# Sliding-window attention in a hybrid decoder layer: the two key blocks of a query block merged into 128 columns a head

## The chip, the cores and the metric

The kernel runs on one core of a Trainium2 chip. The metric is the device time of one execution, in microseconds (us). Engines are named TensorE (PE in the profile; its weight loads are PEld), VectorE (DVE), ScalarE (ACT), GpSimd (POOL) and SyncE (SP), which issues the DMAs.

## The reference

One layer: a norm, a combined projection into a recurrent branch and an attention branch, a gated merge, an MLP and a per-layer embedding. What matters here is the attention, over 512 tokens in 4 blocks of 128, with 16 query heads of width 64 and 4 key and value heads:

```
kb = concat([previous block of k, own block of k])     # 256 keys for 128 queries
s = einsum(q, kb) * 64 ** -0.5
diff = 128 + qi - ci                                   # qi: query 0..127, ci: key 0..255
valid = (diff >= 0) & (diff < 128) & (key exists)
s = where(valid, s, -inf)
m = max(max(s), sink);  e = exp(s - m)
o = (e / (sum(e) + exp(sink - m))) @ vb
```

For a query `qi`, the valid keys are those of the previous block with index above `qi` and those of the own block with index up to `qi`: 128 of the 256, and of each pair of columns (c in the previous block, c in the own block) exactly one. The first block of queries has only its own key block.

## The kernel before

Activations have channels on the partitions and all 512 tokens as columns. Every matmul of a projection is done three times, with operands split into two parts (`mm3`, lines 144 to 147), with 512 columns each. Weights come in units of 128 x 1024 (512 KB), loaded by SyncE and split by ScalarE (`wh`, line 118) and VectorE (`wl`, line 119), up to three units ahead of use.

Attention is a loop (lines 568 to 600) of eight turns `u`: four query blocks for each half of the heads. A turn has two groups `g` of four heads. Between the steps of the attention stand the matmuls of two chunks of the gates' projections (`pgate`), 24 matmuls each, so that TensorE has work while the other engines compute a softmax. In a turn:

- `scores` (line 413) writes 4 heads x 256 columns into the PSUM tile `S`, which has one buffer.
- `softmax_max` (line 426): VectorE adds the mask to the scores, out of PSUM into the SBUF tile `sm` (line 431, two buffers), and takes the maximum over the columns (line 437); four small operations follow (lines 438 to 441).
- `softmax_exp` (line 444): ScalarE, four exponentials, one a head, with sums.
- `softmax_norm` (line 452): VectorE adds and inverts the denominators (lines 455, 456), GpSimd scales the four heads (line 458).
- `p_transpose` (line 462): TensorE transposes each head's 128 x 128 blocks, four heads of a key block into one PSUM tile `ppt` (line 467; the tag `tr` has two buffers, shared with the transposes of the queries).
- `p_evac` (line 471): the first key block's tile is copied to SBUF by ScalarE (line 475), the second's by VectorE (line 477).
- `pv` (line 480): products with v, accumulated over the key blocks; `o_split` (line 491) copies them out on ScalarE and VectorE.

For `u` = 0 and 4 the queries have one key block: there `window(u)` gives 1, the tiles are 128 columns a head, and one tile is transposed and copied. The transposes of the second group of turn `u` come in turn `u + 1`, behind the first gate chunk and ahead of the scores and the products with v. Those of the first group end its own turn.

The order of work on TensorE, ScalarE, SyncE and GpSimd is that of the code (line 80):

```
ctx.enter_context(tc.manual_schedule(engines={E.PE, E.Activation, E.SP, E.Pool}))
```

VectorE is not in that list: the framework orders its work when it builds the program, by priorities and modelled readiness.

The mask, with the rotary tables, is in the table `tab`, one DMA at the start (line 220) behind the loads of x and ahead of the next weights in SyncE's queue.

Of the kernel before, what the change touches and what calls it, by code (L numbers as in the profile page):

```python
# [24 lines left out]

# units of [128, 1024] in the packed weights, in order of use
U_QKV = 0
# [12 lines left out]

# columns of the packed per-channel vectors, 8 each
V_GMIX, V_GMLP, V_GPLE, V_CB, V_BRG, V_BIG, V_LAM, V_CW = 0, 8, 16, 24, 32, 40, 48, 56
N_VEC = 56 + 4 * 8


AHEAD = 3  # weight units split ahead of the one in use
F_BUFS = 24
W_BUFS = 4
N_WARM = 18
CUT = 6  # chunks of a gate projection before the turn of the next queries  # L50
LAG = 2  # chunks between a projection of the recurrent branch and its gates


def weight_order():
    """The units in order of use."""
    def run(u, n=KC):
        return list(range(u, u + n))

    o = run(U_QKV, 12) + run(U_GB) + run(U_GA)
    for m in range(KC + LAG):  # L60
        if m < KC:
            o.append(U_X + m)
        if m >= LAG:
            o.append(U_ATT + m - LAG)
    o += run(U_G) + run(U_RNN) + run(U_OUT) + run(U_MLP, 64) + run(U_PLE, 2) + run(U_PG)
    assert sorted(o + run(U_GATE, 2)) == list(range(N_UNITS))
    return o
# [3 lines left out]
def layer_kernel(ctx, tc, w_all, x_t, p_t, vecs, row, ctab, out_t):  # L71
# [5 lines left out]
    ps = ctx.enter_context(tc.tile_pool(name="ps", bufs=1, space=PSUM))  # L77
    # these engines run their instructions in the order in which they are written here
    E = mybir.EngineType
    ctx.enter_context(tc.manual_schedule(engines={E.PE, E.Activation, E.SP, E.Pool}))  # L80

    def rtile(name):
        """Both parts of four chunks of an activation."""
        return act.tile([P, 4, 2, S], F32R, tag="r", name=name, bufs=4)
# [15 lines left out]

# [1 line left out]
    order = weight_order()  # L102
# [20 lines left out]
    def wload(u):  # L123
        """Unit u, with the units that follow on their way."""
        while u not in ready or (order and len(ready) <= AHEAD):
            wissue()
        return ready.pop(u)

    def split(src, r):
        """r[:, 0] + r[:, 1] = src, both parts exact in 12 bits."""  # L130
        nc.scalar.activation(r[:, 0, :], src, AF.Copy)  # L131
        nc.vector.tensor_tensor(
            out=r[:, 1, :], in0=src, in1=r[:, 0, :].bitcast(F32), op=ALU.subtract
        )

    def split_scaled(src, scale, r):
        """The same for src * scale[partition]."""
        nc.scalar.activation(r[:, 0, :], src, AF.Copy, scale=scale)
        nc.vector.scalar_tensor_tensor(
            out=r[:, 1, :], in0=src, scalar=scale, in1=r[:, 0, :].bitcast(F32),  # L140
            op0=ALU.mult, op1=ALU.subtract,
        )
# [6 lines left out]
    def proj(out, w, acts, ks=range(KC), kcs=KC, w0=0, t=slice(0, S)):  # L149
        """out[c, t] = sum over k of w[k, c] * acts[k, t]."""  # L150
        wh, wl = w
# [4 lines left out]

# [1 line left out]
    vec = const.tile([P, N_VEC], F32, name="vec")  # L158
    nc.scalar.dma_start(vec, vecs)
    tab = const.tile([P, 512], F32, name="tab")  # L160
    rowb = const.tile([P, 144], F32, name="rowb")
    sinkb, qg, kg = rowb[:, 0:16], rowb[:, 16:80], rowb[:, 80:144]
    cosv = tab[:, 0:128].rearrange("p (n d) -> p n d", d=32)
    sinv = tab[:, 128:256].rearrange("p (n d) -> p n d", d=32)
    mask = tab[:, 256:512]
    ident = const.tile([P, P], F32, name="ident")
# [8 lines left out]

# [1 line left out]
    def rms_bcast(sqacc, name):  # L177
        """(mean over channels + eps) ** -0.5 for each token, on every partition."""
        pb = tr_ps(f"pb_{name}")
# [14 lines left out]
    def warm_up():  # L194
        """Keeps the tensor engine busy, and its clock up, until the first loads are in."""
        pw = tr_ps("pw")
        for _ in range(N_WARM):
            nc.tensor.matmul(pw[:, 0:P], ident, ident, start=True, stop=True)
# [6 lines left out]

# [1 line left out]
    xg = rtiles("xg")  # L207
# [13 lines left out]

# [1 line left out]
    att_scope = ExitStack()  # L223
# [4 lines left out]
    def qkv_group(grp, name, after=()):  # L228
        """Projections with tokens on the partitions; after[i]() is emitted behind part i."""
        banks = [mm_ps(f"{name}{n}") for n in range(NB)]  # L230
# [18 lines left out]
    def token_stats():  # L249
        """The mean squares with tokens on the partitions."""  # L250
        ptk = tr_ps("ptk")
# [8 lines left out]

    # rotary tables with the gains folded in: out = t * cc + swap_halves(t) * ss
    def rope_tables(gain, mul, name):
# [21 lines left out]
    def k_side(banks):  # L284
        """Normalized and rotated k of all tokens, v scaled by the norm of its token."""
        kraw = big("kraw")
# [42 lines left out]
    def k_split(kraw, n):  # L329
        # both parts, each doubled, so that a transpose fills all partitions  # L330
        k2 = att.tile([P, 2, 4, 2, HD], F32R, tag="qs", name=f"k2_{n}", bufs=2)
# [29 lines left out]
    def q_scale(u):  # L361
        """(sum of squares over a head + 64 eps mean(x^2)) ** -0.5"""
        n = u % NB
# [51 lines left out]
    def scores(u, g):  # L415
# [8 lines left out]
        return pss  # L424

    def softmax_max(u, g, pss):
        kv = 2 * (u // NB) + g
        w = window(u)[1] * P
        msk = mask[:, 2 * P - w : 2 * P]
        sm = big(f"sm{u}{g}")[:, :, :w]  # L430
        nc.vector.tensor_tensor(out=sm, in0=pss[:, :, :w],
                                in1=msk.unsqueeze(1).broadcast_to([P, 4, w]), op=ALU.add)
        st = att.tile([P, 4, 4], F32, tag="st", name=f"st{u}{g}", bufs=4)
# [28 lines left out]
    def p_transpose(u, g):  # L462
        sm, _ = probs[u, g]
        for kb in range(window(u)[1]):
            pt = tr_ps(f"ppt{u}{g}{kb}")
            for i in range(4):
                nc.tensor.transpose(pt[:, i * P : (i + 1) * P],
                                    sm[:, i, kb * P : (kb + 1) * P], ident)
            p_t_[u, g, kb] = pt

    def p_evac(u, g):
        for kb in range(window(u)[1]):
            prt = ftile(f"pt{u}{g}{kb}")
            if kb == 0:
                nc.scalar.activation(prt, p_t_[u, g, kb], AF.Copy)
            else:
                nc.vector.tensor_copy(prt, p_t_[u, g, kb])
            p_t_[u, g, kb] = prt
# [29 lines left out]

    # c4 = 4 * softplus(-lambda)
    lam = vec[:, V_LAM : V_LAM + 8]  # L510
# [9 lines left out]
    for d in (15, 13, 11, 9, 7, 5, 3):  # L520
        nc.vector.scalar_tensor_tensor(out=pl, in0=pl, scalar=1.0 / d, in1=s2,
                                       op0=ALU.add, op1=ALU.mult)
    # 4 * log1p(e) = 8 * s * (1 + pl)
    nc.vector.scalar_tensor_tensor(out=pl, in0=pl, scalar=1.0, in1=s_,
# [31 lines left out]

# [1 line left out]
    o = [rtile("o0"), rtile("o1")]  # L558
# [43 lines left out]

# [1 line left out]
    rnn = None  # L604
# [21 lines left out]
    def gate_weights(i):  # L626
        """The gates' weights of two chunks."""
        raw = wp.tile([P, S], F32, tag="wr", name=f"wrg{i}", bufs=2)
# [19 lines left out]
    def gate_post(m, xc, both):  # L648
        r, ig = both
        nc.gpsimd.tensor_tensor(out=ig, in0=ig, in1=xc, op=ALU.mult)  # L650
        # t = tanh(-log_a / 2); a = exp(log_a) = 1 - t (1 + a); sqrt(1 - a^2) = sqrt(t) (1 + a)
        nc.scalar.activation(xc, r, AF.Tanh, scale=cs[:, 0, m : m + 1])
# [22 lines left out]
    rnn_scope = ExitStack()  # L675
    later = [[], []]  # what is left of the recurrence, for the next two steps

# [75 lines left out]

# [1 line left out]
    def reload(m):  # L755
# [15 lines left out]

# [1 line left out]
    pr = ple.tile([P, 2, 2, S], F32R, name="pr")  # L773
# [29 lines left out]

# [1 line left out]
    es = []  # L805
# [32 lines left out]

# [1 line left out]
def _units(w):  # L840
    """[1024, 128 n] -> [n, 128, 8 * 128]: unit m holds columns 128 m.., k on the partitions."""
    import numpy as np
# [6 lines left out]
def _pack(i):  # L849
# [19 lines left out]
    for g in range(4):  # L869
# [10 lines left out]
    row = np.concatenate([i["sinks"][0], i["q_gain"][0], i["k_gain"][0]]).reshape(1, 144)  # L880
    # constants of the shapes: rotary angles and the window's mask
    inv = (10000.0 ** (-np.arange(0, 64, 2) / 64)).astype(np.float32)
    ang = np.arange(S, dtype=np.float32)[:, None] * inv[None, :]
    tabs = [t.reshape(NB, P, 32).transpose(1, 0, 2).reshape(P, 128)
            for t in (np.cos(ang), np.sin(ang))]
    qi, ci = np.arange(P)[:, None], np.arange(2 * P)[None, :]
    diff = P + qi - ci
    mask = np.where((diff >= 0) & (diff < P), 0.0, NEG).astype(np.float32)
    ctab = np.concatenate(tabs + [mask], axis=1).astype(np.float32)
    c = np.ascontiguousarray  # L890
# [20 lines left out]
```

## Time and profile before

| | |
|---|---|
| median of 3 runs | 861.26 us (861.09 to 861.58) |
| profiled execution | span 859.3 us from the first to the last instruction; 1.96 us below the median of the runs; no other time of it is recorded |
| busy share of the span | TensorE 99%, its weight loads 81%, VectorE 62%, ScalarE 42%, GpSimd 13% |
| the attention loop | about 83 to 226 us |
| granted TensorE clock | mean 0.999 |

A line of the groups view reads: line, engine, operation, tile written <- tiles read, shapes, count | busy us, mean ns of one | idle us of the engine before them, and what ended it. A line of the chain reads: start, length, what. A matmul's mean is a latency that overlaps its neighbours'. A line of the windows reads: the stretch and its length, then the busy time (and number of instructions) of PE, PEld, DVE, ACT and POOL, the granted clock, the share of the DMA engines and GB/s.

### The profile page before, as it was taken

Reading aid. Unit: us, or ns where it says so; the run is one execution under the profiler, and the core shown is the slowest. Engines: PE = TensorE matmul, PEld = TensorE weight load, DVE = VectorE, ACT = ScalarE, POOL = GpSimd, SP = SyncE. Lnnn points to the kernel's source line nnn. Section 1 sums busy time; section 2 is a strip of 40 time slices with the busy share of each in tenths; the row PEclk is TensorE's granted clock in tenths of the full one; section 3 lists DMA queues with packets and bytes.
Section 4 is the critical chain, followed back from the end, with each engine's and each line's share of the span. In section 5 each row is a group of like instructions: output and inputs, shape, how many; then the busy total and the mean of one; then the engine's idle time right before and its main releaser. Section 6 shows DMA issues by size and latency. Waiting matters only on the chain.

```text
span 859.3 us, 10186 instructions
## 1 busy us (share of the span) xinstructions
PE 851.2 (99%) x3922; PEld 698.9 (81%) x3922; DVE 530.6 (62%) x754; ACT 360.3 (42%) x578; POOL 113.1 (13%) x127
## 2 busy tenths in 40 slices
PE   9999999999999999999999999999999999999997
PEld 8878878777788878888888888888888888888886
DVE  4676787778578886776557643564346434655374
ACT  7342656565557787442434221222122212233431
POOL 2811343323111110000120000000000000002100
PEclk9999999999999999999999999999999999999999
DMA  6332212111223222333342332223223222222231
GB/s 238 122 98 74 74 50 74 63 62 50 75 86 110 74 74 94 117 130 127 136 146 84 98 122 93 81 98 102 98 95 98 98 99 98 98 94 93 84 123 50
DMA packets 25536, 83.35 MB, mean 97 GB/s; under 512 B 2960, under 2 KB 3344, under 8 KB 25488
## 3 DMA queue, kind: packets, MB, share of 16 engines
q1 hardware_dynamic: 25344, 82.66, 28.6%
q8 instruction: 31, 0.51, 0.2%
q14 instruction: 17, 0.14, 0.1%
q10 hardware_dynamic: 144, 0.05, 0.0%
HBM read 80.60 MB, written 2.10 MB: 96 GB/s over the span
## 4 chain that ended last, share of the span: by engine, by line
PE 80%; DVE 8%; ACT 6%; DMA 2%; issue 2%; POOL 1%; SPq 0%; ACTq 0%; DVEq 0%; POOLq 0%
PE pu L145 7%; PE pd L147 7%; PE pu L147 7%; PE pd L145 7%; PE pd L146 7%; PE pu L146 7%; PE pgate L145 3%; PE pgate L146 3%; PE pgate L147 3%; DVE xc L619 3%; DVE wl L119 2%; ACT wh L118 2%; PE S L421 2%; PE ppg L147 2%; PE ppg L145 2%; PE ppg L146 2%
## 5 line engine op out<-in xcount | busy, mean ns | idle before, releaser
L119 DVE TENSOR_TENSOR wl<-wr,wh 128x1024 fp32r<-128x1024 f32 (+1 forms) x143 | 179.8, 1258 | 55.9 <-ACT wh L118 55.8
L118 ACT ACTIVATE wh<-wr 128x1024 fp32r<-128x1024 f32 (+1 forms) x143 | 149.0, 1044 | 120.2 <-PE pd L146 96.2
L145 PE MATMUL pu<-x1g,wh 128*128 128x512 f32 x256 | 100.0, 391 | 0.0
L146 PE MATMUL pu<-x1g,wh 128*128 128x512 f32 x256 | 99.6, 389 | 0.0
L147 PE MATMUL pu<-x1g,wl 128*128 128x512 f32 x256 | 99.6, 389 | 0.0
L145 PE MATMUL pd<-u,wh 128*128 128x512 f32 x256 | 99.6, 389 | 0.0
L146 PE MATMUL pd<-u,wh 128*128 128x512 f32 x256 | 99.6, 389 | 0.0
L147 PE MATMUL pd<-u,wl 128*128 128x512 f32 x256 | 99.6, 389 | 0.0
L204 POOL TENSOR_TENSOR sq<-sq,sq_x 128x512 f32<-128x512 f32 x14 | 18.2, 1298 | 456.8 <-ACT sq_x L202 456.8
L131 ACT ACTIVATE u<-up 128x512 fp32r<-128x512 f32 x32 | 20.2, 632 | 126.5 <-DVE up L790 126.5
L799 DVE TENSOR_TENSOR xr<-pd,xr 128x512 f32<-128x512 f32 x32 | 22.1, 692 | 81.4 <-PE pd L147 81.4
L146 PEld LDWEIGHTS pu<-x1g,wh 128*128 128x128 f32 x256 | 48.1, 188 | 10.2 <-issue 0.2
L145 PEld LDWEIGHTS pu<-x1g,wh 128*128 128x128 f32 x256 | 48.1, 188 | 10.1 <-issue 0.2
L147 PEld LDWEIGHTS pu<-x1g,wl 128*128 128x128 f32 x256 | 48.1, 188 | 10.0
L146 PEld LDWEIGHTS pd<-u,wh 128*128 128x128 f32 x256 | 48.1, 188 | 10.0
L147 PEld LDWEIGHTS pd<-u,wl 128*128 128x128 f32 x256 | 48.1, 188 | 10.0
L145 PEld LDWEIGHTS pd<-u,wh 128*128 128x128 f32 x256 | 48.1, 188 | 9.9
L458 POOL TENSOR_SCALAR sm<-sm,st 128x256 f32<-128x256 f32 (+1 forms) x64 | 39.5, 633 | 96.1 <-DVE st L456 57.9
L145 PE MATMUL pgate<-xg,wh 128*128 128x512 f32 x128 | 51.3, 401 | 0.0
L147 PE MATMUL pgate<-xg,wl 128*128 128x512 f32 x128 | 50.1, 391 | 0.0
L146 PE MATMUL pgate<-xg,wh 128*128 128x512 f32 x128 | 50.1, 391 | 0.0
L789 DVE TENSOR_TENSOR up<-pu,rb_x 128x512 f32<-128x512 f32 x32 | 22.1, 691 | 40.0 <-PE pu L147 40.0
(225 smaller groups left out, 1704.6 us busy)
## 6 DMA issues: line engine op xcount, KB each, us to landing
wr<-in_w_all SPq DMA_DIRECT2D x141, 512.0 KB, 3.3
x<-in_x_t SPq DMA_DIRECT2D x8, 256.0 KB, 4.8
xr<-in_x_t SPq DMA_DIRECT2D x8, 256.0 KB, 3.6
out<-pgt SPq DMA_DIRECT2D x7, 256.0 KB, 2.1
wrg<-in_w_all SPq DMA_DIRECT2D x4, 256.0 KB, 2.9
wr<-in_w_all SPq DMA_DIRECT2D x2, 256.0 KB, 3.2
pk<-in_p_t SPq DMA_DIRECT2D x2, 256.0 KB, 3.7
tab<-in_ctab SPq DMA_DIRECT2D x1, 256.0 KB, 6.2
```

The lines of the kernel that those rows point to most:

```text
L118: nc.scalar.activation(wh[:, c], raw[:, c], AF.Copy)
L119: nc.vector.tensor_tensor(out=wl[:, c], in0=raw[:, c], in1=wh[:, c].bitcast(F32), op=ALU.subtract)
L131: nc.scalar.activation(r[:, 0, :], src, AF.Copy)
L145: nc.tensor.matmul(out, ah, bh, start=start, stop=False)
L146: nc.tensor.matmul(out, ah, bl, start=False, stop=False)
L147: nc.tensor.matmul(out, al, bh, start=False, stop=stop)
L204: nc.gpsimd.tensor_tensor(out=acc, in0=acc, in1=t, op=ALU.add)
L421: nc.tensor.matmul(pss[:, i, :], q_t[u, g][:, i, :], kt[part][:, kv, b0 * P : b0 * P + 256], start=part == 0, stop=part == 1)
L458: nc.gpsimd.tensor_scalar(out=sm[:, i, :], in0=sm[:, i, :], scalar1=den[:, i : i + 1], scalar2=1.0, op0=ALU.mult, op1=ALU.mult)
L619: nc.vector.scalar_tensor_tensor(out=xc[:, sft:], in0=xb[:, : S - sft], scalar=col(V_CW + 8 * j, m), in1=xc[:, sft:], op0=ALU.mult, op1=AL ...
L789: nc.vector.tensor_tensor(out=y, in0=pu, in1=r1, op=ALU.mult)
L799: nc.vector.tensor_tensor(out=x1[m], in0=pd, in1=x1[m], op=ALU.add)
```

## The change

The scores of a two-block group are merged into 128 columns a head: ScalarE copies the own block's columns, VectorE overwrites those where the key index is above the query index with the previous block's (a predicated copy). Maximum, exponentials and scaling then work on 128 columns a head. There is one transposed tile for a group. From it VectorE makes two SBUF tiles, one for each key block, by multiplying with a transposed 0/1 mask. The products with v are as before. For `u` = 0 and 4 a masking add and a copy by ScalarE stay. The table grows from 512 to 768 columns. Comments are removed as well.

```diff
-    tab = const.tile([P, 512], F32, name="tab")
+    tab = const.tile([P, 768], F32, name="tab")
-    mask = tab[:, 256:512]
+    neg, after = tab[:, 256:384], tab[:, 384:512]
+    keep = tab[:, 512:640], tab[:, 640:768]
...
+    def heads4(m):
+        return m.unsqueeze(1).broadcast_to([P, 4, P])
     def softmax_max(u, g, pss):
         kv = 2 * (u // NB) + g
-        w = window(u)[1] * P
-        msk = mask[:, 2 * P - w : 2 * P]
-        sm = big(f"sm{u}{g}")[:, :, :w]
-        nc.vector.tensor_tensor(out=sm, in0=pss[:, :, :w],
-                                in1=msk.unsqueeze(1).broadcast_to([P, 4, w]), op=ALU.add)
+        sm = big(f"sm{u}{g}").rearrange("p a b -> p (a b)")[:, 0 : 4 * P]
+        sm = sm.rearrange("p (i c) -> p i c", c=P)
+        if u % NB:
+            nc.scalar.activation(sm, pss[:, :, P : 2 * P], AF.Copy)
+            nc.vector.copy_predicated(sm, heads4(after.bitcast(mybir.dt.int32)), pss[:, :, 0:P])
+        else:
+            nc.vector.tensor_tensor(out=sm, in0=pss[:, :, 0:P], in1=heads4(neg), op=ALU.add)
...
     def p_transpose(u, g):
         sm, _ = probs[u, g]
-        for kb in range(window(u)[1]):
-            pt = tr_ps(f"ppt{u}{g}{kb}")
-            for i in range(4):
-                nc.tensor.transpose(pt[:, i * P : (i + 1) * P],
-                                    sm[:, i, kb * P : (kb + 1) * P], ident)
-            p_t_[u, g, kb] = pt
+        pt = tr_ps(f"ppt{u}{g}")
+        for i in range(4):
+            nc.tensor.transpose(pt[:, i * P : (i + 1) * P], sm[:, i, :], ident)
+        p_t_[u, g] = pt
     def p_evac(u, g):
-        for kb in range(window(u)[1]):
+        pt = p_t_.pop((u, g))
+        n = window(u)[1]
+        for kb in range(n):
             prt = ftile(f"pt{u}{g}{kb}")
-            if kb == 0:
-                nc.scalar.activation(prt, p_t_[u, g, kb], AF.Copy)
+            if n == 1:
+                nc.scalar.activation(prt, pt, AF.Copy)
             else:
-                nc.vector.tensor_copy(prt, p_t_[u, g, kb])
+                nc.vector.tensor_tensor(out=prt.rearrange("p (i t) -> p i t", t=P),
+                                        in0=pt.rearrange("p (i t) -> p i t", t=P),
+                                        in1=heads4(keep[kb]), op=ALU.mult)
             p_t_[u, g, kb] = prt
...
-    mask = np.where((diff >= 0) & (diff < P), 0.0, NEG).astype(np.float32)
-    ctab = np.concatenate(tabs + [mask], axis=1).astype(np.float32)
+    qi, ci = np.arange(P)[:, None], np.arange(P)[None, :]
+    own = ci <= qi
+    ctab = np.concatenate(tabs + [np.where(own, 0.0, NEG), ~own, ~own.T, own.T],
+                          axis=1).astype(np.float32)
```

## Rows read from the trace of the kernel before

**Rows 1.** The page: span, busy engines, chain by engine.
```profile
span 859.3 us, 10186 instructions
...
PE 851.2 (99%) x3922; PEld 698.9 (81%) x3922; DVE 530.6 (62%) x754; ACT 360.3 (42%) x578; POOL 113.1 (13%) x127
...
PE 80%; DVE 8%; ACT 6%; DMA 2%; issue 2%; POOL 1%; SPq 0%; ACTq 0%; DVEq 0%; POOLq 0%
```

**Rows 2.** Windows: two turns of the loop (u = 2, 3), the stage behind it.
```profile
113.40:131.64 18.24, 17.99 (x98) 13.94 (x98) 14.46 (x30) 11.83 (x31) 6.40 (x9) 1.00 0.18 60
131.64:149.20 17.56, 17.56 (x98) 13.93 (x98) 14.66 (x30) 10.68 (x29) 6.57 (x9) 1.00 0.18 62
226.00:318.00 92.00, 91.83 (x405) 75.40 (x403) 73.18 (x92) 62.50 (x84) 10.22 (x6) 1.00 0.27 92
```

**Rows 3.** The chain that ended last, 117 to 318 us: start, length, what.
```profile
117.88 2.70 POOL sm L458 x4
...
120.62 0.77 PE ppt L467 x5
121.39 0.94 PE S L421 x8
122.33 1.87 PE po L486 x8
...
130.76 0.87 PE ppt L467 x8
...
165.88 0.44 PE ppt L467 x4
...
226.14 0.61 ACT o L494
...
317.91 0.50 PE pg L145
```

**Rows 4.** Groups by line and shape, 82 to 226 us.
```profile
L447 ACT ACTIVATE sm<-sm,st,sc 128x256 f32<-128x256 f32 x48 | 28.2, 591 | 5.9 <-DVE st L441 5.9
...
L467 PE MATMUL ppt<-ident,sm 128*128 128x128 f32 x112 | 16.0, 275 | 0.6
L431 DVE TENSOR_TENSOR sm<-S,tab 128x1024 f32<-128x1024 f32 x12 | 14.6, 1220 | 5.7 <-PE S L421 5.7
L437 DVE TENSOR_REDUCE st<-sm 128x4 f32<-128x1024 f32 x12 | 14.5, 1210 | 0.1
...
L475 ACT ACTIVATE pt<-ppt 128x512 f32<-128x512 f32 x16 | 9.4, 590 | 31.7 <-PE ppt L467 31.6
...
L477 DVE COPY pt<-ppt 128x512 f32<-128x512 f32 x12 | 8.2, 687 | 11.7 <-PE ppt L467 11.7
...
L447 ACT ACTIVATE sm<-sm,st,sc 128x128 f32<-128x128 f32 x16 | 7.7, 487 | 0.0
...
L431 DVE TENSOR_TENSOR sm<-S,tab 128x512 f32<-128x512 f32 x4 | 2.8, 689 | 4.7 <-PE S L421 4.7
L437 DVE TENSOR_REDUCE st<-sm 128x4 f32<-128x512 f32 x4 | 2.7, 679 | 0.0
```

**Rows 5.** Waits of TensorE's weight loads, 82 to 226 us: total, times, longest.
```profile
PEld ppt L467 <- POOL sm L458: 1.6, 5, 0.3
```

**Rows 6.** Timeline around the transposes of the second group, 119 to 131 us.
```profile
119.67 1.72 PE L467 MATMUL ppt<-ident,sm 128*128 128x128 f32 x8
...
121.42 0.69 DVE L477 COPY pt<-ppt 128x512 f32<-128x512 f32 x1 [2.14 <-PE ppt L467]
...
126.27 0.58 ACT L494 ACTIVATE o<-po 128x512 fp32r<-128x512 f32 x1
...
130.49 0.60 ACT L447 ACTIVATE sm<-sm,st,sc 128x256 f32<-128x256 f32 x1 [0.36 <-DVE st L441]
```

**Rows 7.** The page: GB/s in 40 equal slices; the table's DMA.
```profile
GB/s 238 122 98 74 74 50 74 63 62 50 75 86 110 74 74 94 117 130 127 136 146 84 98 122 93 81 98 102 98 95 98 98 99 98 98 94 93 84 123 50
...
tab<-in_ctab SPq DMA_DIRECT2D x1, 256.0 KB, 6.2
```

More of the change, by code (lines that the diff above doesn't have):

```diff
@@ L885, in _pack @@
             for t in (np.cos(ang), np.sin(ang))]
-    qi, ci = np.arange(P)[:, None], np.arange(2 * P)[None, :]
-    diff = P + qi - ci
-    mask = np.where((diff >= 0) & (diff < P), 0.0, NEG).astype(np.float32)
-    ctab = np.concatenate(tabs + [mask], axis=1).astype(np.float32)
+    qi, ci = np.arange(P)[:, None], np.arange(P)[None, :]
+    own = ci <= qi
+    ctab = np.concatenate(tabs + [np.where(own, 0.0, NEG), ~own, ~own.T, own.T],
+                          axis=1).astype(np.float32)
     c = np.ascontiguousarray
```

## The prediction

> **What bounds the kernel now.** I read the page first: TensorE is busy for 851.2 of 859.3 us, VectorE for 530.6, and the chain that ended last is TensorE's for 80% [rows 1]. A share of busy matmul time alone proves little, since matmuls overlap, so the second view was the chain in the stretch that the change touches, the loop over eight query blocks from about 83 to 226 us. There its pieces follow each other without gaps: 0.87 us for eight transposes, 0.44 for four [rows 3], and a next matmul at once. TensorE's queue is full there and its length sets the stage's length. Third, the windows: one turn of the loop takes 17.56 us, all of it TensorE's; the turn before takes 18.24, and TensorE stands idle for a part of it [rows 2]. VectorE is busy for 14.66 of the 17.56, ScalarE for 10.68. Fourth, the waits: in the whole loop TensorE's weight loads wait for GpSimd's normalised probabilities for 1.6 us in five pieces [rows 5], and the chain shows one such place, where GpSimd works until 120.58 and the transposes behind it stretch [rows 3, 6]. Behind the loop the chain runs from 226.14 to 317.91 through ScalarE and VectorE, yet TensorE is busy for 91.83 of 92.00 us [rows 2, 3]: both are about level there. The granted clock is 1.00 in each of these stretches (its upper level, 2.4 GHz), so no clock is to be won.
>
> **TensorE: transposes removed.** There are 8 turns of 2 groups (g = 0, 1) of four heads. The first query block of each half (u = 0 and 4) sees one key block, so 4 groups have four transposes and 12 have eight: 64 + 48 = 112, the count of the row [rows 4]. After the change every group has four. The price of one is the pace and not the 275 ns in the mean column, which is a latency that overlaps: 0.87 us for eight against 0.44 for four, 0.43 us a group [rows 3]. 12 x 0.43 = **5.2 us off TensorE**. Score matmuls and the products with v keep their number and shapes.
>
> The Trainium skill (TensorE: Matmul & The Clock Gate, Part 4: PE-mode transpose) gives about 275 ns for a transpose in a kernel's context; by that the 48 would save 13.2 us, for an end near 848. The row's mean is the same 275 ns, but the chain's pace is 109 ns, and the pace decides.
>
> **VectorE and ScalarE: the merge.** In a 12-group the masking add over 1024 columns (1.220 us) goes. ScalarE copies the own block's 512 columns out of PSUM, nearest row the copy of 512 columns from PSUM, 0.590 us [rows 4]; VectorE then does the predicated copy, which the trace doesn't show. Its bounds: below, 0.69 us, the two-operand masking add of 512 columns from PSUM; above, 1.22 us, should it pass twice, as for 1024 columns. I take 0.69, since it too streams 512 columns and one mask. The maximum falls from 1.210 to 0.679 us [rows 4].
>
> **The exponentials and GpSimd.** Four exponentials fall from 0.591 to 0.487 us each, 0.42 us a group [rows 4]. GpSimd's normalisation halves its columns; I count nothing for that.
>
> **The evacuation.** Before, ScalarE copied one transposed block (0.590) while VectorE copied the other (0.687) [rows 4]. After, VectorE makes both, as two masked multiplies from PSUM, 0.69 us each by the same 512-column row. ScalarE's copy goes.
>
> VectorE's sum for a group: before 1.220 + 1.210 + 0.687 = 3.12 us; after 0.69 + 0.68 + 2 x 0.69 = 2.75; with the slow predicated copy 3.28. Over two groups a turn that makes its 14.66 us into 13.9 or, at worst, 15.0, against a turn of 17.56 - 0.87 = 16.7 us. ScalarE: plus 0.59, minus 0.59, minus 0.42 a group. Both stay under TensorE at either bound, so the merge costs **0 on the path**, covered by the gate projections that run meanwhile. Without the cover each 0.1 us a group would be 1.2 us.
>
> **Waits that move.** ScalarE runs as written, so its new copy stands in line. For g = 0 it follows the exponentials of the previous group. For g = 1 it follows the previous output's copy, which starts at 126.27 [rows 6] and waits for the products with v; what queues behind is the weight split, loaded three units ahead, and the evacuation of the transposed queries. The copy would end near 127, predicated copy and maximum near 128.5, four small operations near 129.5; today this group's exponentials start at 130.49 [rows 6]. The score tile has one buffer, so the next scores (about 131.6 before, 0.4 sooner after) wait for the predicated copy, done some 3 us earlier. At the group that made TensorE wait, the chain of add, maximum, reciprocal, GpSimd gets shorter: two VectorE operations by 1.06 us together, the exponentials by 0.42, while TensorE arrives 0.43 us sooner. The wait of about 0.68 us (18.24 against 17.56) should go, and most of the total of 1.6 [rows 2, 5]. I count **1.3 us** of it, with 0 and 1.6 as ends.
>
> The serial evacuation is the one new step near TensorE: the products with v follow the transposes by one set of scores, 0.94 us in the chain (121.39 to 122.33) [rows 3, 6]. They take eight passes in 1.87 us; the third needs the first masked copy and the seventh the second. Started at once, the copies end after about 0.7 and 1.3 us, against needs at 0.94 + 0.47 = 1.4 and 0.94 + 1.40 = 2.3. There is 0.7 us to spare, and VectorE stands idle for 2.14 us ahead of this place today [rows 6]. Cost taken: 0.
>
> **The table.** It grows from 256 to 384 KB in SP's queue, ahead of the next weights. At the 238 GB/s of the first slice the 128 KB take 0.55 us [rows 7]. Whether the start hides them no row here shows, so I take **0.3 us**, ends 0 and 0.55.
>
> **Sum.** 5.2 + 1.3 - 0.3 = 6.2 us. The profiled span of 859.3 becomes 853.1; the median of the runs is 1.96 us above the span, so 861.26 becomes **855.1 us**. What comes behind the loop hangs on the last output's copy at 226.14, which TensorE's order fixes, so it shifts as a whole.
>
> **The rivals.** *New waits eat part.* The serial evacuation or the late ScalarE copy stops TensorE a little in each of the six turns with two key blocks, or the old wait stays. For: the order of VectorE's work isn't written by hand. Against: 0.7 us to spare. If GpSimd's wait stays and 0.3 us are lost a turn, the gain is 5.2 - 0.3 - 1.8 = 3.1: 858.2 us.
>
> *The gain is not TensorE's to give.* The stage from 226 to 318 us, with its chain on VectorE and ScalarE, would have to end where it ended. For: the chain does go through them. Against: that stage starts at the output's copy, which moves with TensorE, and TensorE has no gap in which the saved time could vanish. Then 861.3 us. The Trainium skill (Perfetto Trace Analysis, Identifying the Most-Contended Engine) holds busy matmul time for a bad measure and weight-load time for a better one. By that, 13.93 of 17.56 us, 79%, leaves TensorE room and speaks for this rival; the gapless chain speaks against.
>
> *Slower: VectorE comes late to the masked copies.* The place is the products with v, six times. TensorE stops as soon as VectorE starts more than 0.7 us after the transposes; it decides the sign from 0.7 + 6.2 / 6 = 1.7 us. With three 512-column operations of 0.69 in front, 2.07 us, it stops 1.4 us six times, 8.4 us: 861.26 - 6.2 + 8.4 = 863.5 us. Against: today's copy of the same tile starts 0.03 us after the transposes end at 121.39 [rows 3, 6].
>
> **How the numbers follow.** My forecast has 0.62, the partial gain 0.20, no gain 0.08, slower 0.10. Lowest: 5.2 + 1.6 and nothing lost is 854.5, and the runs spread by 0.5 us with the slack of the other small stalls beside it: 853.6. Above, the range reaches to 858.4, over the partial case's 858.2; outside are no gain, slower, and tails. A difference of 0.2%, 1.7 us, is about what a measurement here can tell from none; faster holds the first two cases, 0.82; same 0.08; slower 0.10.
>
> **What would show it.** Right: 64 transposes instead of 112; the pieces of eight gone from the chain; a turn of about 16.7 us; TensorE's loads waiting for GpSimd for under 0.5 us in the loop; the predicated copy near 0.7 us; no wait of the products with v for the masked copies. Wrong: TensorE waiting for the masked multiplies or for the score tile; the predicated copy at 1.2 us with VectorE above 15 us a turn; a later start of the first query projection; or the loop shorter while the stage from 226 us on grows by as much.

## The result and the profile after

The changed kernel takes 855.74 us (median of 4 runs, 854.91 to 857.01), the one before 861.17 us on the same chip (860.89 to 861.58): a ratio of 0.9935, 95% interval 0.9923 to 0.9947, faster by 5.4 us. The profiled execution has a span of 853.7 us, where 853.1 was forecast. Lines of the changed kernel from the softmax on are numbered 1 to 10 higher than before (the transposes are L474, the predicated copy L438).

The page after, in answer to [rows 1]: span, busy engines, chain by engine, the table's DMA.
```profile
span 853.7 us, 10088 instructions
...
PE 844.9 (99%) x3874; PEld 692.7 (81%) x3874; DVE 526.9 (62%) x766; ACT 354.9 (42%) x578; POOL 103.1 (12%) x127
...
PE 87%; DVE 5%; ACT 3%; DMA 2%; issue 1%; POOL 1%; SPq 0%; ACTq 0%; POOLq 0%; DVEq 0%
...
tab<-in_ctab SPq DMA_DIRECT2D x1, 384.0 KB, 7.5
```
TensorE has 48 instructions less, VectorE 12 more with 3.7 us less work. TensorE's share of the chain rises from 80 to 87%.

Windows, as in [rows 2]: the turns u = 2 and 3, and the stage behind the loop. Columns: stretch, its length, busy us (instructions) of TensorE, its loads, VectorE, ScalarE, GpSimd; TensorE's granted clock; DMA share; GB/s.
```profile
113.01:129.65 16.64, 16.64 (x91) 13.05 (x90) 14.05 (x33) 9.81 (x27) 4.93 (x9) 1.00 0.22 75
129.65:146.28 16.63, 16.63 (x90) 13.04 (x90) 13.99 (x33) 9.83 (x27) 4.91 (x9) 1.00 0.19 63
220.00:312.00 92.00, 91.68 (x404) 75.32 (x402) 72.88 (x91) 62.23 (x83) 10.20 (x6) 1.00 0.27 92
```
Both turns now last 16.6 us, where [rows 2] had 18.24 and 17.56: the second lost 0.93 us, two groups' transposes, the first 1.60, that and its wait. The start of each turn's first scores in the two traces (as the chain has it), and in the last column that of the first projection behind the loop:

| | u=0 | 1 | 2 | 3 | 4 | 5 | 6 | 7 | behind the loop |
|---|---|---|---|---|---|---|---|---|---|
| before | 82.71 | 97.18 | 113.40 | 131.64 | 149.20 | 166.32 | 182.54 | 200.78 | 217.19 |
| after | 82.75 | 97.23 | 113.01 | 129.65 | 146.28 | 162.91 | 178.69 | 195.33 | 210.81 |

The eight turns give 6.42 us: eleven groups near 0.46 each, and two waits of 0.67, in the turns u = 2 and 6. The twelfth group comes behind the loop, and there the change loses. From the first projection behind the loop to the last products with v it was 6.94 us, with eight transposes, and is 7.36, with four.

The chain after, to lay beside [rows 3]:
```profile
129.21 0.44 PE ppt L474 x4
129.65 0.92 PE S L422 x8
...
136.03 0.44 PE ppt L474 x4
...
210.66 0.69 DVE gate L573
211.35 0.60 DVE pt L485
...
212.89 1.17 POOL sm L466
...
214.10 0.33 PE ppt L474
```
In the loop only pieces of four transposes are left, followed by scores at once. At 210.66 us the chain leaves TensorE: VectorE evacuates a gate projection and makes two masked copies ahead of the last group's reciprocal (its sum stands between the two), GpSimd normalises late, and the transposes come one by one, each 0.33 us.

The groups of line and shape, to lay beside [rows 4] (busy us, mean ns of one | idle before):
```profile
L485 DVE TENSOR_TENSOR pt<-ppt,tab 128x512 f32<-128x512 f32 x24 | 15.8, 685 | 3.8 <-PE ppt L474 3.8
...
L474 PE MATMUL ppt<-ident,sm 128*128 128x128 f32 x64 | 10.3, 276 | 0.3 <-POOL sm L466 0.3
L438 DVE COPY_PREDICATED sm<-tab,S 128x512 f32<-128x512 int32 x12 | 8.9, 745 | 1.6 <-ACT sm L437 1.2
```
And the waits, 82 to 230 us, with the answer to [rows 5] in the last line:
```profile
DVE st L463 <- ACT st L458: 11.6, 8, 2.5
...
DVE pt L485 <- PE ppt L474: 3.8, 3, 1.8
...
PEld ppt L474 <- POOL sm L466: 1.3, 4, 0.7
```
All four of the waits for GpSimd lie in the last group. No product with v waits for a masked copy. VectorE's own idle time has moved: it waited 10.4 us for scores and 2.1 us for exponentials before, and waits 11.6 us for exponentials now.

### The profile page after: what moved, and what is told of

Same layout as the page of the kernel before. It is cut to its first block, busy times and chain, and to the rows that moved or that the text cites. A ratio compares the mean times of both kernels' runs of the same rounds, so it can differ in the third digit from the quotient of the medians.

```text
span 853.7 us, 10088 instructions
## 1 busy us (share of the span) xinstructions
PE 844.9 (99%) x3874; PEld 692.7 (81%) x3874; DVE 526.9 (62%) x766; ACT 354.9 (42%) x578; POOL 103.1 (12%) x127
## 4 chain that ended last, share of the span: by engine, by line
PE 87%; DVE 5%; ACT 3%; DMA 2%; issue 1%; POOL 1%; SPq 0%; ACTq 0%; POOLq 0%; DVEq 0%
PE pu L145 7%; PE pd L147 7%; PE pu L147 7%; PE pd L145 7%; PE pd L146 7%; PE pu L146 7%; PE pgate L145 4%; PE pgate L146 3%; PE pgate L147 3%; PE S L422 2%; PE ppg L147 2%; PE ppg L145 2%; PE ppg L146 2%; PE pgl L147 2%; PE pout L147 2%; PE pout L145 2%
## 5 line engine op out<-in xcount | busy, mean ns | idle before, releaser
L466 POOL TENSOR_SCALAR sm<-sm,st 128x128 f32<-128x128 f32 x64 | 28.3, 461 | 92.4 <-DVE st L464 46.9
```

The costliest lines, as they stand in the source:

```text
L466: nc.gpsimd.tensor_scalar(out=sm[:, i, :], in0=sm[:, i, :], scalar1=den[:, i : i + 1], scalar2=1.0, op0=ALU.mult, op1=ALU.mult)
```

## The experiments

In each expectation, A and its rival are those of that run. All ratios are to the kernel before on the same chip, with 95% intervals. A table at the end of this section has the stretches of all the traces side by side.

**The changed kernel again**, on another chip, beside which the next three stand.

> The changed kernel as it is, beside the three below on the same chip, for a basis and for the spread of its runs. Either theory: about 855.7 us, 5.4 us under the kernel before.

855.88 us against 861.05, ratio 0.9943 (0.9930 to 0.9957), span 853.2. The result holds.

**The transposes put back.** The changed kernel issues each group's transposes as often as before, into the same tile.
```
-        for i in range(4):
+        for i in [0, 1, 2, 3] * window(u)[1]:
             nc.tensor.transpose(pt[:, i * P : (i + 1) * P], sm[:, i, :], ident)
```


> The changed kernel with the four transposes of each two-block group made twice into the same tile: TensorE's count is back at 112, all else as changed. Theory A: the gain is the length of TensorE's queue; the time rises by 12 x 0.43 = 5.2 us, less what the last group's wait swallows (0.4), to about 860.5, and against the kernel before only the removed waits, about 0.5 to 1.3 us, remain. Theory B: the gain comes from the shorter work on VectorE, ScalarE and GpSimd; then the time stays near 856.

860.68 us, ratio 0.9995 (0.9986 to 1.0004): the gain is gone. The merge, its shorter softmax and the masked copies were all still there. The medians put 4.8 us on the 48 transposes; the sum had 5.2. In the traces the eleven groups of the loop cost 5.07 us (133.13 against 128.06), 0.46 each, and the twelfth group's disappear in its wait for GpSimd. Against the kernel before, the loop is still 1.35 us shorter: the two waits are gone here too. That does not show in the time, since the last group takes 0.37 us more and this execution came to its first scores 0.54 us later, which is within the spread of the traces (82.20 to 83.86 us).

**The transposes alone taken away**, from the kernel before. The second key block's tile is here a copy of the first's, so the attention is not that of the reference.
```
-        for kb in range(window(u)[1]):
+        for kb in range(1):
             pt = tr_ps(f"ppt{u}{g}{kb}")
...
-                nc.vector.tensor_copy(prt, p_t_[u, g, kb])
+                nc.vector.tensor_copy(prt, p_t_[u, g, 0])
```


> The kernel before with the transposes of the second key block left out: VectorE copies the first block's transposed tile instead, from SBUF, behind ScalarE's copy. Scores, mask, maximum, exponentials and scaling keep their 256 columns a head, so the attention's output is that of wrong probabilities for one block; the amount of the other work is as before. Theory A: TensorE has 48 transposes less, 5.2 us, but the softmax chain is as long as before while TensorE arrives 0.43 us sooner, so the three places where it waits for GpSimd wait longer, 0.4 us each, and new ones may come: 861.2 - 5.2 + 1.3 = about 857.3 us. Theory B (the shorter softmax chain brings nothing of its own): about 855.7 to 856, as the changed kernel.

857.87 us, ratio 0.9965 (0.9953 to 0.9978): 3.2 of some 5 us. The waits in its loop, 82 to 320 us:
```profile
PEld ppt L467 <- POOL sm L458: 3.0, 9, 0.6
PEld pg L145 <- ACT r L644: 2.2, 2, 1.7
PEld po L486 <- DVE pt L477: 1.4, 5, 0.3
```
The loop gains 4.1 us by its trace (130.40 against 134.48). With the softmax still 256 columns wide, TensorE runs into GpSimd in nine places instead of five, 3.0 us instead of 1.6. Another 1.4 us of waits belong to the edit alone, which puts VectorE's copy behind ScalarE's. And 1.2 us are lost again behind the loop, where the loads wait 2.2 us for the gates instead of 1.0. So in the loop the shorter queue gives 4.1 of the change's 6.4 us by itself, the shorter softmax 1.35 (the run before), and about 1.0 comes only with both; how much of that is due to this edit's own serial copy stays open.

**ScalarE's copy of the second group's scores ahead of the output's copy.**
```
         s1 = scores(u, 1)
+        softmax_max(u, 1, s1)
         if u:
             o_split(u - 1, pv(u - 1))
-        softmax_max(u, 1, s1)
```


> ScalarE copies the own block's scores of the second group ahead of the previous output's copy, instead of behind it. Theory A: what is left of the wait for GpSimd sits at the last group's transposes (about 1.3 us of TensorE's weight loads at 214 us), and is late because this copy stands behind an output's copy that waits for the products with v. Then the exponentials of that group start about 1.5 to 2 us sooner, the wait goes, and the time falls by 0.7 to 1.3 us, to about 854.7. Theory B: the lateness comes from VectorE, which does the masked multiplies ahead of the reciprocals, or from GpSimd's own pace; then the wait stays and the time stays within 0.3 us of the changed kernel's.

855.35 us, ratio 0.9935 (0.9922 to 0.9947), alone hardly to be told from the changed kernel. In its trace the wait for GpSimd is gone: the last group's exponentials start at 208.26 us instead of 209.43, and the stretch from the first projection behind the loop to the products with v takes 6.16 us instead of 7.36. Two other things change with it: the last group's reciprocal comes 1.92 us sooner and not only 1.17, since it is now ahead of the gate evacuation and the masked copies on VectorE, and no weight split falls into GpSimd's normalisations. Of the 1.2 us, 0.5 are lost again behind it, in waits for the gates of the recurrence (82 to 320 us, the changed kernel first, then this one):
```profile
PEld pg L145 <- ACT r L654: 1.2, 2, 0.7
```
```profile
PEld pg L145 <- ACT r L654: 1.8, 2, 1.3
```
The chain shows why. The recurrence there waits for a weight unit that lands 4.09 us after VectorE releases its buffer in the changed kernel and 4.54 in this one:
```profile
278.64 4.09 DMA wr<-in_w_all
```
```profile
277.58 4.54 DMA wr<-in_w_all
```
Before it was 3.72. The gates' small weights take turns with the big ones in the same two buffers.

**The gates' weights in buffers of their own**, in the changed kernel, with the copy first as well, and in the kernel before.
```
-        raw = wp.tile([P, S], F32, tag="wr", name=f"wrg{i}", bufs=2)
+        raw = ftile(f"wrg{i}")
```


> The changed kernel with the raw gate weights of the recurrent branch in a tile of their own, not in one of the two buffers through which the weight units are loaded. Theory A: behind the loop the path goes through ScalarE, VectorE and two weight loads that are issued late because the gate weights hold a buffer (3.7 to 4.9 us each, longer in some executions), and part of what the loop saves is lost there, as TensorE then waits 0.3 to 0.8 us for a gate at about 312 us; then that wait goes and the time falls by 0.3 to 0.6 us, to about 855.4, with a smaller spread. Theory B: TensorE is the bound of that stage and its short wait is not worth anything: no change, 855.9.

854.70 us, ratio 0.9919 (0.9906 to 0.9933).

> The scores' copy ahead of the output's copy, and the gate weights in a tile of their own. Theory A: 1.2 us at the last group's transposes and 0.5 to 0.8 at the gates of the recurrent branch, so about 854.2. Theory B (neither wait is on the path): 855.4 to 855.9, as either alone.

853.00 us (852.54 to 853.68), ratio 0.9903 (0.9889 to 0.9917): the best version of the study, ahead of both kernels. All that TensorE's loads still wait for a producer between 82 and 320 us is this:
```profile
PEld S L422 <- ACT qt L407: 0.5, 1, 0.5
```

> The kernel before with the raw gate weights of the recurrent branch in a tile of their own. Theory A (the two late weight loads hold TensorE only where it comes early to that stage, as in the changed kernel): here TensorE waits under 0.2 us for them, so 0 to 0.4 us, about 860.9. Theory B (they are worth the same in both kernels): 1.2 us, 860.0.

860.65 us, ratio 0.9995 (0.9986 to 1.0003), no difference that can be measured. By the traces the stage from the last products with v to the next projections takes 95.3 us before, 94.5 with the buffers apart; 95.5 in the changed kernel, 94.5 with them apart. So by one trace each the shared buffers cost 0.8 us before the change and 1.0 after it: the change did not bring this cost, and lost about 0.3 us by it (0.4 in its second trace).

**The merge made dearer.** First the masked copies: those of the second group three times.
```
-                nc.vector.tensor_tensor(out=prt.rearrange("p (i t) -> p i t", t=P),
-                                        in0=pt.rearrange("p (i t) -> p i t", t=P),
-                                        in1=heads4(keep[kb]), op=ALU.mult)
+                for _ in range(3 if g else 1):
+                    nc.vector.tensor_tensor(...)
```


> The changed kernel with each of the two masked multiplies of a second group made three times, 24 more of about 0.6 us start to start. Theory A (the place named for the slower rival: the products with v wait once the masked tiles are late by more than about 0.7 us): the first tile is ready some 1.9 us after the transposes against a need at 1.4, the second, with pieces of the rotary work between, at some 4.5 against 2.3; TensorE stops about 2.2 us in each of the six turns with two key blocks, less where VectorE is not free, and the time rises by 10 to 14 us, to 866 to 870. Theory B (this evacuation is hidden, as the merge is): within 1 us of 855.9.

875.80 us, ratio 1.0168 (1.0150 to 1.0187).
```profile
PEld po L497 <- DVE pt L486: 20.2, 11, 2.5
...
PE po L497 <- DVE pt L486: 10.5, 11, 1.7
```
The wait stands where the slower rival put it, at the products with v, but in five places and not six: behind the loop, where half a projection stands between the last group's transposes and the products with v, the stretch keeps its 7.34 us. Five turns grow by 3.0 to 4.3 us, 17.2 in all. Four more multiplies of 0.685 us are 2.7 us a group; less the 0.7 us to spare, that would be 2.0. In the trace of the turn u = 3 two pieces of the rotary work, 0.68 and 0.41 us (at 142.29 and 143.49 us), stand among the multiplies, where the changed kernel has them behind: 3.1 us by this estimate, against 3.4 measured. Why one turn grows by 4.3 stays open.

Then the predicated copy twice, as if it passed twice over its columns.
```
-            nc.vector.copy_predicated(sm, heads4(after.bitcast(mybir.dt.int32)), pss[:, :, 0:P])
+            for _ in range(2):
+                nc.vector.copy_predicated(sm, heads4(after.bitcast(mybir.dt.int32)),
+                                          pss[:, :, 0:P])
```


> The changed kernel with each predicated copy made twice, 12 more of 0.745 us, 8.9 us of VectorE. Theory A (the merge lies under TensorE's gate projections): no wait in the turns of the loop; only the last group's transposes, already late, come 0.6 to 0.75 us later, so 855.9 becomes 856.5 at most. Theory B (VectorE is close to the bound in the loop): the turns grow by up to 1.2 us each and the time by 4 to 9 us, to 860 or more.

867.80 us, ratio 1.0076 (1.0062 to 1.0089): slower than before, though VectorE stayed below TensorE in every turn. Its window of the turn u = 3:
```profile
130.52:148.71 18.19, 18.16 (x88) 13.26 (x88) 14.95 (x35) 9.70 (x27) 4.97 (x9) 1.00 0.17 58
```
A turn of 18.19 us in which VectorE works for 14.95. The loop is 6.9 us longer than in the changed kernel, and the last group behind it 5.3. My reading was that 0.75 us a group is over some margin of the softmax's way to GpSimd, perhaps 0.7 us a turn. The next run was to measure that margin with a smaller step: an extra predicated copy over one head's 128 columns.
```
             nc.vector.copy_predicated(sm, heads4(after.bitcast(mybir.dt.int32)), pss[:, :, 0:P])
+            nc.vector.copy_predicated(sm[:, 0], after.bitcast(mybir.dt.int32), pss[:, 0, 0:P])
```


> The changed kernel with the predicated copy and one more of it over a single head's 128 columns, about 0.25 us more of VectorE a group, 0.5 us a turn. Theory A (a ring: VectorE works, waits about 1.6 us a turn for the exponentials, works on; what it can take on before TensorE waits is only its wait for TensorE, 0.69 us a turn in the trace of the changed kernel): it fits, so the turns stay at 16.6 us and the time rises by at most 0.6 us, at the last group, from 855.9. Theory B (each microsecond more on VectorE costs what it cost when the whole copy was doubled, 12 us for 8.9): 3 us of work more, about 4 us, 860.

864.80 us, ratio 1.0048 (1.0033 to 1.0064). 12 x 0.300 = 3.6 us of VectorE's work cost 9.5 us of span. The theory of a margin fell: a step two fifths as large costs four fifths as much. The compiled programs gave the next theory. VectorE's instructions are ordered when the kernel is built, not as written, and with one more instruction in each group the order is another (48 of the other 766 stand elsewhere): the gate evacuation comes ahead of the maximum, and both masked multiplies ahead of the last small operations. So the step was cut to next to nothing, 8 columns; its list of VectorE instructions is that of the 128-column kernel, one for one.
```
-            nc.vector.copy_predicated(sm[:, 0], after.bitcast(mybir.dt.int32), pss[:, 0, 0:P])
+            nc.vector.copy_predicated(sm[:, 0, 0:8], after[:, 0:8].bitcast(mybir.dt.int32),
+                                      pss[:, 0, 0:8])
```


> The changed kernel with the extra predicated copy of the run before cut from 128 columns to 8: VectorE's order of instructions is the same as with 128 columns, one for one, while the added work falls from 0.300 us a group to a fixed cost of perhaps 0.1 us or less (estimate: the four-column operations of this loop). Theory A (the order costs: with the extra instruction the gate evacuation and the masked multiplies come ahead of the maximum's small operations, so the second group's exponentials start late): the time stays near that of the 128-column copy, 864.8, less at most 12 x 0.2 = 2.4 us, so 862 to 865, a turn near 17.6 us or more, and TensorE's transposes wait for GpSimd by over 4 us in the loop. Rival B (the added VectorE work costs, the order does not): 12 x 0.1 us is a third of the 3.6 us, so 856 to 858, and the wait for GpSimd is under 2 us.

864.59 us, ratio 1.0043 (1.0028 to 1.0058). The extra copy takes 0.162 us, 1.9 us in all, and costs 9.0 us of span. The order costs, and hardly the work: from 8 to 128 columns, 1.7 us more work, nothing measurable is added. No run has the new order without an added instruction, so what the 1.9 us themselves cost is not shown apart. The same place in the two timelines, the changed kernel first:
```profile
129.40 1.16 PE L422 MATMUL S<-kt,qt 128*128 128x256 f32 x8
...
130.59 0.15 DVE L449 TENSOR_TENSOR st<-rowb,st 128x4 f32<-128x4 f32 x1
130.67 0.68 DVE L485 TENSOR_TENSOR pt<-ppt,tab 128x512 f32<-128x512 f32 x1
130.78 0.49 ACT L455 ACTIVATE sm<-sm,st,sc 128x128 f32<-128x128 f32 x1 [2.21 <-DVE st L449]
...
133.50 1.42 POOL L466 TENSOR_SCALAR sm<-sm,st 128x128 f32<-128x128 f32 x4 [5.75 <-ACT sm L437]
...
134.80 1.22 DVE L119 TENSOR_TENSOR wl<-wr,wh 128x1024 fp32r<-128x1024 f32 x1
135.87 0.60 PE L474 MATMUL ppt<-ident,sm 128*128 128x128 f32 x4
```
```profile
130.67 1.16 PE L422 MATMUL S<-kt,qt 128*128 128x256 f32 x8
...
131.72 0.68 DVE L486 TENSOR_TENSOR pt<-ppt,tab 128x512 f32<-128x512 f32 x1
...
132.38 0.68 DVE L486 TENSOR_TENSOR pt<-ppt,tab 128x512 f32<-128x512 f32 x1
...
133.25 0.16 DVE L450 TENSOR_TENSOR st<-rowb,st 128x4 f32<-128x4 f32 x1
133.43 0.49 ACT L456 ACTIVATE sm<-sm,st,sc 128x128 f32<-128x128 f32 x1 [3.60 <-DVE st L450]
...
136.16 2.38 POOL L467 TENSOR_SCALAR sm<-sm,st 128x128 f32<-128x128 f32 x4 [6.07 <-ACT sm L437]
...
137.01 1.28 DVE L119 TENSOR_TENSOR wl<-wr,wh 128x1024 fp32r<-128x1024 f32 x1
137.13 0.49 PE L475 MATMUL ppt<-ident,sm 128*128 128x128 f32 x3
...
138.59 0.33 PE L475 MATMUL ppt<-ident,sm 128*128 128x128 f32 x1 [0.96 <-POOL sm L467]
```
In the changed kernel the last small operation comes ahead of the second masked multiply, and the exponentials start 1.38 us after the scores (130.78 - 129.40). In the other order the gate evacuation, the maximum and both multiplies come first, and they start 2.76 us after. Then GpSimd's four normalisations take 2.38 us instead of 1.42, because VectorE's weight split now falls into them. They end at 134.9 in the changed kernel, 0.95 us ahead of the transposes; in the other they end at 138.5, and TensorE waits. TensorE's loads wait for GpSimd 12 times, 8.6 us in all; four of these waits, 4.2 us, lie in the last group. The loop is 4.3 us longer than in the changed kernel, and the last group alone 4.2, of which about 1.1 us are TensorE's clock: after two idle stretches of 3.2 us together the granted clock falls to 0.50, and five matmuls take 0.43 us a piece instead of 0.23, a sixth 0.37:
```profile
224.00:226.00 2.00, 2.00 (x6) 1.59 (x5) 1.04 (x2) 0.00 (x0) 0.00 (x0) 0.50 0.14 53
```

**Both, the copy first and the predicated copy twice.**

> The scores' copy ahead of the output's copy, and each predicated copy made twice. In the trace with that copy first, VectorE waits 1.3 us a turn for TensorE (0.70 and 0.61), and doubling adds about 1.36. Theory A (the ring, with the late place of the copy in it): it just about fits, so 855.4 becomes 856 to 858. Theory B (the place of the copy is not part of what bounds the turn): as with the copy behind, 12 us more, 867.

862.59 us, ratio 1.0018 (1.0009 to 1.0027): between the two expectations. The earlier copy takes 4.6 us back in the loop and nothing at the last group, which still costs 5.3 us more than in the changed kernel. A part of that is TensorE's clock. Windows of 2 us at the last group (columns as above):
```profile
216.00:218.00 2.00, 0.24 (x2) 0.00 (x0) 0.34 (x2) 2.00 (x8) 0.01 (x1) 1.00 0.00 0
218.00:220.00 2.00, 0.53 (x2) 0.33 (x2) 1.23 (x1) 0.33 (x1) 2.00 (x3) 0.71 0.00 0
220.00:222.00 2.00, 2.00 (x6) 1.45 (x6) 0.99 (x2) 0.00 (x0) 0.44 (x2) 0.50 0.36 131
222.00:224.00 2.00, 2.00 (x6) 1.56 (x5) 0.29 (x1) 0.00 (x0) 0.00 (x0) 0.50 0.00 0
224.00:226.00 2.00, 2.00 (x7) 1.19 (x8) 0.00 (x1) 0.00 (x0) 0.00 (x0) 0.58 0.00 0
226.00:228.00 2.00, 2.00 (x9) 0.62 (x10) 0.69 (x1) 0.10 (x1) 0.00 (x0) 1.00 0.00 0
```
TensorE works for 0.77 of 4 us while it waits for GpSimd, the granted clock falls to 0.50 (its lower level, 1.2 GHz), and the chain's matmuls then take 0.43 us a piece instead of 0.23, eleven of them: 11 x 0.20 = 2.2 us lost behind waits of 3.2 us in two pieces.

**All the traces side by side.** From the starts of matmuls, in us: the loop runs from the first scores to the first projection behind it, the last group from there to the last products with v, the stage from there to the next projections.

| | loop | last group | stage behind |
|---|---|---|---|
| before | 134.48 | 6.94 | 95.28 |
| changed | 128.06 | 7.36 | 95.53 |
| changed, again | 128.06 | 7.37 | 95.66 |
| transposes put back | 133.13 | 7.31 | 95.34 |
| before, transposes alone taken away | 130.40 | 7.13 | 96.44 |
| copy first | 128.06 | 6.16 | 96.05 |
| gates' weights apart | 128.05 | 7.34 | 94.52 |
| both of these | 128.05 | 6.16 | 94.52 |
| before, gates' weights apart | 134.51 | 6.94 | 94.52 |
| masked multiplies three times | 145.26 | 7.34 | 96.65 |
| predicated copy twice | 134.95 | 12.66 | 95.09 |
| 128 columns more | 132.42 | 11.87 | 95.84 |
| 8 columns more | 132.39 | 11.56 | 95.23 |
| copy first, predicated copy twice | 130.36 | 12.67 | 94.84 |

Most of these edits also draw a new order of VectorE's work, the transposes put back the least of those that touch the loop: 9 of 766 instructions stand elsewhere.

## Why the prediction was right, point by point

The sum said 6.2 us and the span gave 5.6. Term by term:

- **Transposes, 5.2 us.** Right: 0.43 to 0.47 a group in the turns, and 5.07 for the loop's eleven groups when they are put back (4.8 for all by the medians). 64 transposes in the trace, as said. The pace of 0.44 us for four [rows 3] held in the changed kernel's chain; the 275 ns of the Trainium skill (TensorE: Matmul & The Clock Gate, Part 4: PE-mode transpose) is again only the mean column, 276.
- **The wait for GpSimd, 1.3 us.** Right in the turns, 2 x 0.67, though for a cause that the prediction did not see, and missed in one place. It had the chain of softmax steps getting shorter. The trace of before shows what the wait was made of: in both places a weight split of VectorE holds up the first of GpSimd's four normalisations, 1.33 us instead of 0.47 (last section). Without these 0.86 us they would have ended near 119.7 us (estimate), when TensorE came to its transposes at 119.67 [rows 6]. In the changed kernel they run from 116.81 to 118.25 us, nearly all ahead of the split at 118.11 and a microsecond before the transposes. How much of that is the shorter chain and how much the place of the split is not shown apart. The prediction looked at the group that had made TensorE wait and not at the last one, which has less cover: half a projection stands between its transposes and those of its neighbour, 3.2 us in the copy-first trace, and not scores and a whole projection, 6.8 us (129.05 to 135.87 us in the loop). There the twelfth group, which should have given 0.43, lost 0.42: 0.9 us under the sum. The copy-first run shows the cause that the prediction itself named, ScalarE's copy in line behind the output's copy, with its exponentials 1.2 us too late. By that they came behind other work of VectorE (0.75 us more) and into a weight split, beside which the first normalisation took 1.16 us instead of 0.37.
- **The exponentials no later than before.** Wrong by 1.2 us: the small operations were to be done near 129.5 and end at 130.7, since the gate evacuation and a masked multiply stand ahead of them. The exponentials start at 130.78, not before the 130.49 of [rows 6], while TensorE is 1.99 us further on. It cost nothing here only because the rest of the way had become shorter.
- **The merge, 0 us.** Right at its price: 0.745 us for the predicated copy (0.69 taken), VectorE at 14.05 and 13.99 us a turn (13.9 forecast). "Both stay under TensorE at either bound" is a weak reason, though, as the 8-column run shows: with no more work a turn than that bound allows, that kernel's span was 9.0 us longer. Whether a single predicated copy of 1.22 us would have cost anything stays open, since the copy made twice also changed the order.
- **The serial evacuation, 0 us.** Right: no product with v waited. The mechanism of the slower rival is real, as the tripled multiplies show, in five places where the prediction had six, and its condition was not met.
- **The table, 0.3 us.** It took 7.5 us to land instead of 6.2 [rows 7]. The first scores start 0.04 us later, but from 82.20 to 83.86 us in the traces with the longer table and from 82.65 to 82.96 in the three without: the term is too small to be told from this spread, and stays open.
- **The stage behind the loop shifts as a whole.** Nearly: 95.5 instead of 95.3 us from the last products with v, 0.3 us less gained, beside a weight unit that lands 0.37 us later (4.09 against 3.72).

6.42 in the turns, minus 0.42 at the last group, minus 0.3 in the stage, minus 0.04 at the start is 5.7, which is the span's 5.6 within the rounding. The gapless chain decided, as the run with the transposes put back shows. The rule by which TensorE had room, that of the Trainium skill (Perfetto Trace Analysis, Identifying the Most-Contended Engine) to go by the share of weight-load time, here 79%, did not.

The range held, and for a part by luck: no sentence of the prediction priced the order of VectorE's work, which the diff does not state. In the order of the 8-column run, with 1.9 us more work, the change came out slower than the kernel before. And the two waits of 0.67 us that went stood beside weight splits, whose place the prediction had not looked at.

## What to carry to other kernels

Read a full queue from a gapless chain and price what leaves it at its pace, 0.43 us a group here; then look for the one place that has less cover than the others, here the last group, where this change lost 0.9 us of its gain and the runs with another order lost 4.2 to 5.3 us each. An engine's busy share (14 of 16.6 us) says nothing of its order: follow the softmax's way to GpSimd instruction by instruction, and note how much time is left at its end (0.95 us). Where a builder orders an engine's work, adding an instruction to double a cost also draws a new order; run the same order with next to no work beside it, or the cost is put down to the wrong thing.

## What the hardware showed that was not expected

GpSimd stood still while VectorE split a weight unit. Of the four normalisations at 150.14 us in the changed kernel, beside a split of 1.22 us at 150.51, three took 0.37 us and one 1.41, 1.04 more; at 133.5, beside the predicated copy and the maximum, none did (minimum, median and maximum of four):
```profile
L466 POOL TENSOR_SCALAR sm<-sm,st x4: 367/370/1410, 150.1 to 152.2; 128x128 f32<-128x128 f32 x4
```
```profile
L466 POOL TENSOR_SCALAR sm<-sm,st x4: 372/373/377, 133.5 to 134.5; 128x128 f32<-128x128 f32 x4
```
The Trainium skill (SBUF — State Buffer, Who interferes with whom) says that a VectorE instruction with two inputs in SBUF and a GpSimd instruction that reads SBUF exclude each other until the first is done. The split reads two SBUF tiles, the predicated copy and the maximum of these rows do not, and the trace agrees.

The trace shows the same at the old wait for GpSimd. The split and the four normalisations of [rows 3] in the kernel before, then the four of the changed kernel's last group, beside a split at 212.62:
```profile
117.64 1.22 DVE L119 TENSOR_TENSOR wl<-wr,wh 128x1024 fp32r<-128x1024 f32 x1
...
L458 POOL TENSOR_SCALAR sm<-sm,st x4: 475/475/1333, 117.9 to 120.1; 128x256 f32<-128x256 f32 x4
```
```profile
L466 POOL TENSOR_SCALAR sm<-sm,st x4: 365/365/1157, 212.9 to 214.7; 128x128 f32<-128x128 f32 x4
```

A short predicated copy is nearly all fixed cost: 0.162 us for 8 columns, 0.300 for 128, 0.745 for 512, which is about 1.15 ns for a further column and 0.15 us besides. And a wait of TensorE costs more than its length once the granted clock falls: after 3.2 us in two pieces it was at 0.50 for eleven matmuls in one run and for more than five in another, while in the changed kernel, with waits up to 0.7 us in the same place, it stayed at 1.00.
